# One token tile's up rows summed by TensorE, no fifth dense tile, and most expert activations made in the up stage

## The chip, the cores and the metric

The kernel runs on one core of one Trainium2 chip. The metric is the device time of one execution in microseconds; the number quoted for a kernel is the median over its timed runs. Beside these, one execution is recorded by the hardware profiler; its span runs from the first to the last instruction.

The core's engines work in parallel, each from its own in-order queue: TensorE (PE; its weight loads are PEld), VectorE (DVE), ScalarE (ACT), GpSimd (POOL) and SyncE (SP), which here only starts DMA transfers.

## The reference

One decoder layer for 1024 tokens of 1024 features, in fp32. A mixer (gated short convolution beside dilated attention, merged by gates) is followed by a retrieval layer over 16384 experts, and by a last normalisation:

```python
h = h + hybrid_mixer(rms_norm(h, norm_mix[layer]), ...)
h = h + peer_ffn(rms_norm(h, norm_ffn[layer]), w_query, sub_keys, expert_down, expert_up)
return rms_norm(h, final_norm)

# peer_ffn: each of 8 heads picks 16 experts for each token: 128 rows of each table
idx, gates = ...                     # (token, 128) expert numbers and their softmax weights
a = gelu(einsum('cd,ced->ce', xc, expert_down[ic]))    # 128 dot products per token
out = einsum('ce,ced->cd', gc * a, expert_up[ic])      # weighted sum of 128 up rows per token
```

The table `expert_down` (`down`) and the table `expert_up` (`up`) hold 16384 rows of 1024 numbers, 64 MiB each.

## The kernel before, in words

Tokens are handled in two halves of 512, and in tiles of 128 tokens (0 to 3 in the first half, 4 to 7 in the second). The whole program is written as Python generators that yield a cost; the instructions of two of them, a main line and a side line, are interleaved by these costs and the numbers `PACE_B`, `PACE_C`, `PACE_D`. A scheduler of the framework then fixes the order in each engine's queue, by its own estimate of when things are ready.

The main line: the mixer of the first half and its expert scores (**mixer 0**); the mixer of the second half and its scores (**mixer 1**); then `dense()`, which treats the experts of the second half without any gather. `dense()` has two stages:

- the **hidden stage**: `hidden(q)` multiplies the weights of 512 experts (`down_t`) with all 512 tokens and applies gelu; a group q takes 4 x 8 x 3 = 96 matmuls of 512 columns, because each fp32 product is made of three f32r products of a high and a low part (`mm3`, L176 to L178; `weights()` loads 512 KB into `raw`, ScalarE casts it to `hi`, VectorE subtracts to get `lo`, L163 to L167). There are 32 groups. The first `STORED` = 27 results are sent to DRAM (`a_d`), the next `HOLD` = 4 stay. Meanwhile `routes()` makes the gates: for each tile it chooses the experts on VectorE (`choose`), then `build` makes one-hot matrices of four tokens at a time (`oa`, `ob`), multiplies them on TensorE (`psg`), copies them on ScalarE (`stg`) and stores a full gate matrix in DRAM (`g_d`). `RATE_G` sets how fast the builder goes beside the hidden groups;
- the **up stage**: for each group q, `fetch(q)` reads the activations back, `weigh(q)` multiplies them with the gates `gg` read from `g_d` and splits them into `hh` and `hl`, and the rows of `up` are loaded (`rawu`), split (`uh`, `ul`) and multiplied, 24 matmuls for each tile. Six of the sums stay in PSUM for the whole stage (`held`), the others are added to SBUF by VectorE (`rest`, L1089).

The side line, `experts()`, treats the tiles of the first half by gathers: POOL fetches one of the 128 expert rows of each token (512 KB for a tile of 128 tokens) by an indirect DMA into one of `ROWS` = 4 buffers; VectorE makes the dot product (`row`, L875) or adds the scaled row to `acc` (`rowu`, L891). So a tile takes 128 gathers with dots and 128 with row sums. Tile 1 is an exception: its dots are made this way, but its up rows go through `dense()` as a fifth tile (`XT`, `given`), which takes its gates from the side line and needs `gx`, `xh`, `xl` in each up step.

POOL's queue holds all gathers and the small loads of the side line, SP's queue all other transfers.

Of the kernel before, what the change touches and what calls it, by code (L numbers as in the profile page):

```python
# [8 lines left out]
F32 = mybir.dt.float32  # L9
# [8 lines left out]
P = 128  # L18
# [15 lines left out]
PACE_B = 2.0  # L34
PACE_D = 2.0
PACE_C = 2.2
RATE_G = 0.8
STORED = 27
HOLD = 4
# [9 lines left out]
TILES = (4, 5, 6, 7, 1)  # L49
STB = 2  # L50
XT = (1,)
GXB = 2
XHB = 1
# [12 lines left out]
def hybrid_layer(ctx, tc, x, xT, pos, rotc, norm_mix, w_proj, w_v, conv_w, w_conv_out, w_attn_out,  # L66
                 gate_bias, w_out, norm_ffn, w_query, sub_keys, down, down_t, up, final_norm, out):
# [83 lines left out]
    s_d = dram.tile([3, P, 16, P], F32, name="s_d")  # L151
    a_d = dram.tile([STORED, P, NB, TH], F32, name="a_d")
    g_d = dram.tile([(TH + len(XT) * P) // TC, P, P, TC], F32, name="g_d")
# [540 lines left out]
    def tail(half, tiles, h1, sts, after):  # L694
# [32 lines left out]
        kept = tiles if half else [t for t in tiles if t == 0]  # L727
# [3 lines left out]
        for hc in range(16):  # L731
# [11 lines left out]
            if sent:  # L743
                others = w2k.tile([P, 3, P], F32, tag="t0", name="others")[:, 0:len(sent)]
                S.copy(others, pk[:, len(kept):nt])
                nc.sync.dma_start(s_d[sent[0] - 1:sent[-1], :, hc].rearrange("t p k -> p t k"), others)
# [86 lines left out]
    def stored(tt):  # L833
        part = {}

        def column(hc):
            if hc % 2 == 0:
                part[0] = ex.tile([P, 2, P], F32, tag="sv", bufs=2, name="sv")
                SIDE.dma_start(part[0], s_d[tt - 1, :, hc:hc + 2])
# [4 lines left out]
    later = [None] + [choose(stored(tt), False, picked) for tt in (1, 2, 3)]  # L844
# [14 lines left out]
    xready = {}  # L859

    def experts():
        for tt in ORDER:
            r = slice(tt * P, tt * P + P)
            if tt:
                for _ in later[tt]:
                    pass
            idx, gate = picked[tt]
            ut = ex.tile([P, D], F32, tag="ut", name="ut")
            SIDE.dma_start(ut, u2_d[r])
            a = ex.tile([P, P], F32, tag="a", name="a")  # L870
            for e in range(P):
                row = gt.tile([P, D], F32, tag="row", name="row")
                G.indirect_dma_start(out=row, out_offset=None, in_=down,  # L873
                                     in_offset=bass.IndirectOffsetOnAxis(ap=idx[:, e:e + 1], axis=0))
                V.tensor_tensor_reduce(out=row, in0=row, in1=ut, scale=1.0, scalar=0.0, op0=ALU.mult,  # L875
                                       op1=ALU.add, accum_out=a[:, e:e + 1])
                yield 1.0
            S.activation(a, a, AF.Gelu)
            if tt in XT:
                ax = ex.tile([P, P], F32, tag=f"ax{tt}", name="ax")  # L880
# [295 lines left out]
```

## Time and profile before

| | us |
|---|---|
| median of 3 timed runs (lowest, highest) | 3424.61 (3417.29, 3427.93) |
| the profiled execution, its own time | 3433.88 |
| its span, first to last instruction | 3432.1 |
| TensorE busy in it | 3274.4 |
| VectorE busy | 2760.1 |
| ScalarE busy | 1461.7 |
| POOL busy | 1190.2 |
| bytes moved by DMA | 948.08 MB |

Busy time is the time in which an engine executes at least one instruction. Matmuls follow each other in a pipeline, so what TensorE gets done is read from how many start in a stretch, not from its busy share alone. The granted TensorE clock has two levels, 1.2 and 2.4 GHz; its mean share over the span is 0.984.

### The profile page before, as it was taken

Reading aid. Unit: us, or ns where it says so; the run is one execution under the profiler, and the core shown is the slowest. Engines: PE = TensorE matmul, PEld = TensorE weight load, DVE = VectorE, ACT = ScalarE, POOL = GpSimd, SP = SyncE. Lnnn points to the kernel's source line nnn. Section 1 sums busy time; section 2 is a strip of 40 time slices with the busy share of each in tenths; the row PEclk is TensorE's granted clock in tenths of the full one; section 3 lists DMA queues with packets and bytes.
Section 4 is the critical chain, followed back from the end, with each engine's and each line's share of the span. In section 5 each row is a group of like instructions: output and inputs, shape, how many; then the busy total and the mean of one; then the engine's idle time right before and its main releaser. Section 6 shows DMA issues by size and latency. Waiting matters only on the chain.

```text
span 3432.1 us, 47074 instructions
## 1 busy us (share of the span) xinstructions
PE 3274.4 (95%) x15923; PEld 2685.0 (78%) x15923; DVE 2760.1 (80%) x5646; ACT 1461.7 (43%) x3271; POOL 1190.2 (35%) x944
## 2 busy tenths in 40 slices
PE   7999999999989999988999989999999999999998
PEld 6787888887767777767777878888877878787787
DVE  4333355689999889988999999998887878888887
ACT  3544444443334353333226777787632222222222
POOL 0000000014543345555434443464544334444342
PEclk9999999999989999989999999999999999999999
DMA  4233335668888678988889898999989989999895
GB/s 129 77 119 110 103 127 191 244 230 305 302 279 276 227 260 307 342 316 292 315 316 328 329 330 334 344 340 336 348 301 336 334 316 338 326 340 333 309 350 208
DMA packets 364307, 948.08 MB, mean 276 GB/s; under 512 B 33952, under 2 KB 127648, under 8 KB 356640
## 3 DMA queue, kind: packets, MB, share of 16 engines
q1 hardware_dynamic: 232016, 465.27, 38.9%
q0 software_dynamic: 132048, 479.78, 38.8%
q8 instruction: 126, 2.06, 0.2%
q14 instruction: 117, 0.96, 0.1%
HBM read 843.15 MB, written 95.49 MB: 273 GB/s over the span
## 4 chain that ended last, share of the span: by engine, by line
PE 32%; DVE 20%; DMA 14%; issue 11%; POOL 5%; ACT 1%; SPq 0%; DVEq 0%; POOLq 0%; ACTq 0%
DVE row L875 6%; PE ps L178 6%; PE ps L176 6%; PE ps L177 6%; DMA row<-in_down,idx 5%; DMA rowu<-in_up,idx 4%; DMA gg<-g_d 4%; DVE lo L167 3%; POOL row L873 3%; POOL rowu L889 2%; PE held L177 2%; PE held L178 2%; PE held L176 2%; DVE acc L891 1%; PE psg L975 1%
## 5 line engine op out<-in xcount | busy, mean ns | idle before, releaser
L873 POOL DMA_INDIRECT row<-in_down,idx x512 | 640.9, 1252 | 885.2 <-DVE a L875 465.6
L889 POOL DMA_INDIRECT rowu<-in_up,idx x384 | 525.8, 1369 | 621.1 <-DVE acc L891 499.0
L165 ACT CAST hi<-raw 128x1024 fp32r<-128x1024 f32 x368 | 387.6, 1053 | 746.0 <-PE ps L177 541.1
L875 DVE CUSTOM_DVE_ANT_0 row<-row,ut 128x1024 f32<-128x1024 f32 x512 | 618.8, 1215 | 79.2 <-DMA row<-in_down,idx 74.0
L167 DVE TENSOR_TENSOR lo<-raw,hi 128x1024 fp32r<-128x1024 f32 x368 | 448.1, 1218 | 247.9 <-ACT hi L165 238.6
L178 PE MATMUL ps<-vhi,lo 128*128 128x512 f32 (+1 forms) x1408 | 535.4, 382 | 33.5 <-DVE lo L167 33.4
L176 PE MATMUL ps<-vhi,hi 128*128 128x512 f32 (+1 forms) x1408 | 530.6, 377 | 10.8 <-ACT hi L165 6.7
L891 DVE SCALAR_TENSOR_TENSOR acc<-rowu,a,acc 128x1024 f32<-128x1024 f32 x384 | 491.2, 1279 | 59.7 <-DMA rowu<-in_up,idx 57.3
L177 PE MATMUL ps<-vlo,hi 128*128 128x512 f32 (+1 forms) x1408 | 528.9, 376 | 0.0
L178 PE MATMUL ps<-uhi,lo 128*128 128x512 f32 x1024 | 409.1, 400 | 4.2 <-DVE lo L167 4.2
L176 PE MATMUL ps<-uhi,hi 128*128 128x512 f32 x1024 | 407.6, 399 | 5.7 <-ACT uhi L181 3.1
L177 PE MATMUL ps<-ulo,hi 128*128 128x512 f32 x1024 | 409.1, 400 | 0.5 <-DVE ulo L182 0.5
L178 PEld LDWEIGHTS ps<-vhi,lo 128*128 128x128 f32 x1408 | 269.1, 191 | 87.4 <-DVE lo L167 44.4
L176 PEld LDWEIGHTS ps<-vhi,hi 128*128 128x128 f32 x1408 | 269.7, 192 | 58.9 <-ACT hi L165 10.9
L177 PEld LDWEIGHTS ps<-vlo,hi 128*128 128x128 f32 x1408 | 269.1, 191 | 45.1
L177 PE MATMUL held<-ul,hh 128*128 128x512 f32 x624 | 247.0, 396 | 11.1 <-DVE ul L182 10.9
L178 PE MATMUL held<-uh,hl 128*128 128x512 f32 x624 | 244.0, 392 | 2.5 <-DVE hl L182 2.5
L176 PEld LDWEIGHTS ps<-uhi,hi 128*128 128x128 f32 x1024 | 194.1, 190 | 52.1 <-ACT uhi L181 5.2
L176 PE MATMUL held<-uh,hh 128*128 128x512 f32 x624 | 233.3, 393 | 0.0
L178 PEld LDWEIGHTS ps<-uhi,lo 128*128 128x128 f32 x1024 | 194.3, 190 | 47.9 <-DVE lo L167 6.4
L177 PEld LDWEIGHTS ps<-ulo,hi 128*128 128x128 f32 x1024 | 194.1, 190 | 45.1 <-issue 3.0
L181 ACT CAST hh<-ga 128x512 fp32r<-128x512 f32 x128 | 71.4, 618 | 353.0 <-DVE ga L990 348.9
(347 smaller groups left out, 5947.8 us busy)
## 6 DMA issues: line engine op xcount, KB each, us to landing
raw<-in_w_proj SPq DMA_DIRECT2D x128, 512.0 KB
raw<-in_down_t SPq DMA_DIRECT2D x128, 512.0 KB
rawu<-in_up SPq DMA_DIRECT2D x128, 512.0 KB
g_d<-stg SPq DMA_DIRECT2D x80, 512.0 KB
gg<-g_d SPq DMA_DIRECT2D x32, 1024.0 KB
a_d<-ga SPq DMA_DIRECT2D x27, 1024.0 KB
ga<-a_d SPq DMA_DIRECT2D x27, 1024.0 KB
raw<-in_w_query SPq DMA_DIRECT2D x48, 512.0 KB
```

Of the source, the lines that this page charges most:

```text
L165: S.copy(hi, raw)
L167: V.tensor_tensor(lo, raw, hi.bitcast(F32), op=ALU.subtract)
L176: PE.matmul(ps, l[0], r[0], start=first, stop=False)
L177: PE.matmul(ps, l[0], r[1], start=False, stop=False)
L178: PE.matmul(ps, l[1], r[0], start=False, stop=last)
L181: S.copy(hi, src)
L873: G.indirect_dma_start(out=row, out_offset=None, in_=down, in_offset=bass.IndirectOffsetOnAxis(ap=idx[:, e:e + 1], axis=0))
L875: V.tensor_tensor_reduce(out=row, in0=row, in1=ut, scale=1.0, scalar=0.0, op0=ALU.mult, op1=ALU.add, accum_out=a[:, e:e + 1])
L889: G.indirect_dma_start(out=row, out_offset=None, in_=up, in_offset=bass.IndirectOffsetOnAxis(ap=idx[:, e:e + 1], axis=0))
L891: V.scalar_tensor_tensor(acc, row, a[:, e:e + 1], acc, op0=ALU.mult, op1=ALU.add)
L975: PE.matmul(ps[:, t], ob[:, t], oa[:, t], start=True, stop=True)
```

## The change

- The fifth dense tile is gone: `given`, `gx`, `xh`, `xl` are removed, `dense()` has four tiles. The side line takes tile 1's up rows by gathers and row sums like the others.
- Tile 0's up rows are gathered too, but by token instead of by rank: `turn_over` transposes its weights and expert numbers, so that one gather brings the 128 rows of one token, one per partition. `summed` lets TensorE add them: for four tokens at a time it multiplies the rows by a matrix `z` that is zero but for one column, into a strip of 32 output columns for each of the four, both halves of the features, 256 fp32 matmuls in all, over two PSUM tiles (`upacc`). Its rows use the four gather buffers and pairs of the large buffers (`rowb`) in turn. The up stage is not written before this sum is done (`while "done" not in place`).
- The side line's order is now given by `STEPS`: the dots of tiles 0, 1 and 2, then the sums of tiles 0 (TensorE), 1 and 2 (VectorE), then tile 3's dots and sums.
- `STORED` is 8 and `HOLD` is 2: 10 hidden groups are made in the hidden stage, 22 in the up stage, each one step before it is used.
- The gates `gg` have one buffer of their own, not one of the ten large ones; the scores of three tiles of the second half go through DRAM (`s_d`); `weigh` works on halves of 256 tokens; the rows of `up` are laid out on the host (`up_s`) so that a load is contiguous in each partition.
- The paces: the side line goes faster beside mixer 1, the builder faster beside the hidden groups.

```diff
-PACE_B = 2.0
-PACE_D = 2.0
-PACE_C = 2.2
-RATE_G = 0.8
-STORED = 27
-HOLD = 4
+PACE_B = 1.55
+PACE_D = 1.55
+PACE_C = 1.75
+RATE_G = 1.3
+STORED = 8
+HOLD = 2
...
-TILES = (4, 5, 6, 7, 1)
+STEPS = ((0, 0), (1, 0), (2, 0), (0, 1), (1, 1), (2, 1), (3, 0), (3, 1))
+TILES = (4, 5, 6, 7)
 STB = 2
-XT = (1,)
-GXB = 2
-XHB = 1
+SUMMED = 0
+ZK = 2
...
-            if tt in XT:
-                ax = ex.tile([P, P], F32, tag=f"ax{tt}", name="ax")
-                V.tensor_tensor(ax, a, gate, op=ALU.mult)
-                xready[tt] = (idx, ax)
...
+            if tt == SUMMED:
+                while not place:
+                    yield 1.0
+                acc = ex.tile([P, D], F32, tag="acc", name="acc")
+                yield from summed(*turned[tt], acc, r)
...
+        def add(s, rows):
+            z = zs[s // ZK % 2]
+            c0 = 31 + 32 * (s % ZK) - s
+            first = None
+            for n in range(2):
+                for j in (3, 0, 1, 2):
+                    with tc.issue_after(first.ins) if first else ExitStack():
+                        m = PE.matmul(part[n][32 * j:32 * j + 32], z[:, j, c0:c0 + 32], rows[j][:, n * TH:n * TH + TH],
+                                      start=s == 0, stop=s == 31)
+                    first = first or m
+
+        for s in range(32):
+            if s % ZK == 0:
+                S.copy(zs[s // ZK % 2][:, :, 31::32][:, :, 0:ZK], columns[:, :, s:s + ZK])
+            if s % 2:
+                pair = [m8.tile([P, 2, D], F32, tag="big", name="rowb") for _ in range(2)]
+                rows = [pair[j // 2][:, j % 2] for j in range(4)]
+            else:
+                rows = [gt.tile([P, D], F32, tag="row", name="rowu") for _ in range(4)]
+            for j in range(4):
+                t = 32 * j + s
+                G.indirect_dma_start(out=rows[j], out_offset=None, in_=up,
+                                     in_offset=bass.IndirectOffsetOnAxis(ap=iT[:, t:t + 1], axis=0))
+            if waiting:
+                add(*waiting.pop())
+            waiting.append((s, rows))
+            yield 4.0
...
-            gg = m8.tile([P, TH // TC, NB, TC], F32, tag="big", name="gg")
-            nc.sync.dma_start(gg, g_d[:TH // TC, :, NB * q:NB * q + NB].rearrange("c j i t -> j c i t"))
+            gg = up_p.tile([P, TH // TC, NB, TC], F32, tag="gg", bufs=1, name="gg")
+            nc.sync.dma_start(gg, g_d[:, :, NB * q:NB * q + NB].rearrange("c j i t -> j c i t"))
...
         for _ in builder:
             yield 0.0
+        while "done" not in place:
+            next(side)
...
-                    r0 = (NB * q + ii) * P
-                    nc.sync.dma_start(raw, up[r0:r0 + 2 * P, n * TH:n * TH + TH].rearrange("(a p) d -> p a d", a=2))
+                    nc.sync.dma_start(raw, up_s[(NB * q + ii) // 2, n])
```

Two places show where the instructions stand now. The first is TensorE's queue at the end of the hidden stage of the kernel before: `ps` are hidden matmuls (the last of L176 to L178), `psg` the gate builds, and the numbers tell buffers apart.

```order
L178 MATMUL ps<-vhi_12767,lo 128x512
L975 MATMUL psg<-oa,ob 128x128 x4
L176 MATMUL ps<-vhi_12767,hi 128x512
L177 MATMUL ps<-vlo_12769,hi 128x512
L178 MATMUL ps<-vhi_12767,lo 128x512
L176 MATMUL ps<-vhi_12766,hi 128x512
L177 MATMUL ps<-vlo_12768,hi 128x512
```

In the changed kernel the same stage ends with these rows; `upacc` are the sums over strips (8 matmuls for four tokens), `rowu` and `rowb` their gathered rows, `ps_t` the transposes with which the last tile's gates begin, `held` the first matmuls of the up stage.

```order
L178 MATMUL ps<-vhi_13012,lo 128x512
L1038 MATMUL psg<-oa,ob 128x128 x8
L944 MATMUL upacc<-rowu,z_13826 32x512 x8
L944 MATMUL upacc<-rowb,z_13826 32x512 x8
L1038 MATMUL psg<-oa,ob 128x128 x24
L944 MATMUL upacc<-rowu,z_13827 32x512 x8
L944 MATMUL upacc<-rowb,z_13827 32x512 x8
L1038 MATMUL psg<-oa,ob 128x128 x32
L1015 MATMUL ps_t<-ident,e_17743 128x128 x2
L1015 MATMUL ps_t<-ident,ge 128x128
L1038 MATMUL psg<-oa,ob 128x128 x128
L176 MATMUL held_18912<-uh,hh 128x512
```

Before, the last builds stood between hidden matmuls, and more hidden ones followed them; now the `upacc` sums stand in the queue in sixteens, and the last 184 builds have no hidden matmul beside or behind them.

The other place is VectorE's queue in one step of the up stage, from the product with the gates (`ga<-ga,gg`) on; `row,a` is a dot of a gathered row, `a` its second half. Before:

```order
L990 TENSOR_TENSOR ga_26741<-ga_26741,gg_26743 128x512 x4
L182 TENSOR_TENSOR ul_26326<-rawu_26323,uh_26325 128x1024
L1089 TENSOR_TENSOR rest_22594<-rest_22594,psu_26289 128x512
L182 TENSOR_TENSOR ul_26416<-rawu_26413,uh_26415 128x1024
L1089 TENSOR_TENSOR rest_22594<-rest_22594,psu_26290 128x512
L875 ISA row_23887,a_21908<-row_23887,ut_21906 128x1024
L875 ISA a_21908 128x1
L875 ISA row_23896,a_21908<-row_23896,ut_21906 128x1024
```

In the changed kernel, with the last `lo` split of a hidden group ahead of the product:

```order
L167 TENSOR_TENSOR lo_24374<-raw_24370,hi_24372 128x1024
L1056 TENSOR_TENSOR ga_23981<-ga_23981,gg_24152 128x4x256 x2
L887 ISA row_22674,a_22287<-row_22674,ut_22285 128x1024
L887 ISA a_22287 128x1
L887 ISA row_22683,a_22287<-row_22683,ut_22285 128x1024
L887 ISA a_22287 128x1
L182 TENSOR_TENSOR hl_24155<-ga_23981,hh_24154 128x4x256 x2
L887 ISA row_22706,a_22287<-row_22706,ut_22285 128x1024
L887 ISA a_22287 128x1
L182 TENSOR_TENSOR ul_24256<-rawu_24253,uh_24255 128x1024
L1146 TENSOR_TENSOR rest_18914<-rest_18914,psu_24174 128x512
```

The `lo` splits of the hidden groups have moved into the up stage, between the dots, and each dot waits in this queue for its gathered row.

## Rows read from the trace of the kernel before

**Rows 1.** The page: busy time by engine; the chain that ended last.
```profile
PE 3274.4 (95%) x15923; PEld 2685.0 (78%) x15923; DVE 2760.1 (80%) x5646; ACT 1461.7 (43%) x3271; POOL 1190.2 (35%) x944
PE 32%; DVE 20%; DMA 14%; issue 11%; POOL 5%; ACT 1%; SPq 0%; DVEq 0%; POOLq 0%; ACTq 0%
```

**Rows 2.** Busy time by stretch: four stages, three of 100 us.
```profile
core 0: us, PE busy (x) PEld busy (x) DVE busy (x) ACT busy (x) POOL busy (x), PEclk, DMA share, GB/s
0.00:750.00 750.00, 720.71 (x3650) 589.20 (x3651) 382.44 (x910) 338.77 (x659) 5.30 (x17) 0.99 0.43 142
750.00:1580.00 830.00, 772.15 (x3921) 625.60 (x3920) 750.81 (x1822) 318.42 (x608) 385.27 (x325) 0.96 0.85 292
1580.00:2480.00 900.00, 860.80 (x4381) 723.79 (x4380) 844.66 (x1876) 563.42 (x1666) 415.31 (x305) 0.99 0.90 329
2480.00:3432.00 952.00, 920.71 (x3976) 746.39 (x3974) 782.24 (x1040) 241.10 (x339) 384.36 (x299) 0.99 0.88 318
1700.00:1800.00 100.00, 92.16 (x397) 73.67 (x397) 93.09 (x287) 28.36 (x36) 39.99 (x35) 1.00 0.89 314
2700.00:2800.00 100.00, 100.00 (x438) 82.02 (x437) 83.01 (x125) 25.56 (x34) 36.44 (x30) 1.00 0.91 329
3000.00:3100.00 100.00, 99.89 (x435) 81.05 (x434) 83.81 (x104) 20.94 (x29) 43.68 (x35) 1.00 0.95 345
```

**Rows 3.** Groups by line: busy us, mean ns of one, idle before, releasers.
```profile
L873 POOL DMA_INDIRECT row<-in_down,idx x512 | 640.9, 1252 | 885.2 <-DVE a L875 465.6 <-DVE tv L762 115.6 <-issue 35.6
L875 DVE CUSTOM_DVE_ANT_0 row<-row,ut 128x1024 f32<-128x1024 f32 x512 | 618.8, 1215 | 79.2 <-DMA row<-in_down,idx 74.0 <-issue 4.0 <-DMA ut<-u_d 0.9
L167 DVE TENSOR_TENSOR lo<-raw,hi 128x1024 fp32r<-128x1024 f32 x368 | 448.1, 1218 | 247.9 <-ACT hi L165 238.6 <-DMA raw<-in_w_proj 4.2 <-PE pst L548 2.1
L891 DVE SCALAR_TENSOR_TENSOR acc<-rowu,a,acc 128x1024 f32<-128x1024 f32 x384 | 491.2, 1279 | 59.7 <-DMA rowu<-in_up,idx 57.3
L975 PE MATMUL psg<-oa,ob 128*128 128x128 f32 x1280 | 162.0, 279 | 8.5 <-ACT stg L977 5.9 <-DVE ob L968 1.9 <-ACT ob L973 0.7
L977 ACT COPY stg<-psg 128x128 f32<-128x128 f32 x640 | 126.0, 286 | 61.8 <-PE psg L975 29.9 <-DMA g_d<-stg 22.9 <-issue 7.8
L966 ACT ACTIVATE ob<-iota,sT 128x128 f32<-128x128 f32 x320 | 103.9, 416 | 0.2
L967 ACT ACTIVATE ob<-ob,ones 128x512 f32<-128x512 f32 x80 | 60.7, 764 | 0.1
L1089 DVE TENSOR_TENSOR rest<-rest,psu 128x512 f32<-128x512 f32 x120 | 80.4, 679 | 2.0 <-PE psu L178 2.0
```

**Rows 4.** TensorE in time: start us, us, line, out<-in, count.
```profile
166.46 1.09 PE L504 MATMUL pv<-pts,v_t 128*64 128x128 f32 x16
...
508.71 1.02 PE L244 MATMUL prs<-diag,ones 128*128 128x512 f32 x2
509.81 0.39 PE L178 MATMUL ps<-uhi,lo 128*128 128x512 f32 x1
```

**Rows 5.** POOL's gathers by stage: of `in_down` (L873), then of `in_up` (L889).
```profile
1580.00:2480.00 900.00, 267.47 (x213) 0.99 0.90 329
2480.00:3432.00 952.00, 165.14 (x128) 0.99 0.88 318
...
1580.00:2480.00 900.00, 147.27 (x91) 0.99 0.90 329
2480.00:3432.00 952.00, 215.81 (x165) 0.99 0.88 318
```

**Rows 6.** Who waited for whom in the up stage: us, times, longest.
```profile
DVE ga L990 <- DMA gg<-g_d: 73.3, 26, 8.4
```

**Rows 7.** All engines in order of time around 1749 us.
```profile
1748.07 1.22 DVE L875 CUSTOM_DVE_ANT_0 row<-row,ut 128x1024 f32<-128x1024 f32 x1 [2.50 <-DMA row<-in_down,idx]
1749.22 1.22 DVE L167 TENSOR_TENSOR lo<-raw,hi 128x1024 fp32r<-128x1024 f32 x1
1750.49 0.50 PE L178 MATMUL ps<-vhi,lo 128*128 128x512 f32 x1 [2.68 <-DVE lo L167]
```

More of the change, by code (lines that the diff above doesn't have):

```diff
@@ L724, in tail @@
             result["next"] = mixer(1)
-        kept = tiles if half else [t for t in tiles if t == 0]
+        kept = [t for t in tiles if t == 0]
         sent = [t for t in tiles if t not in kept]
@@ L856, in finish, with new_row @@
             queue.dma_start(out[r, c], acc[:, c])
[L859 removed]
+    place = {}
+    spare = []
+    count = [0]
+    def new_row(name):
+        pools = [gt] * ROWS + spare
+        pool = pools[count[0] % len(pools)]
+        count[0] += 1
+        return pool.tile([P, D], F32, tag="row", name=name)
     def experts():
[L862 removed]
+        values, turned = {}, {}
+        for tt, side_up in STEPS:
             r = slice(tt * P, tt * P + P)
[L864 to L894 removed]
@@ new lines, in experts @@
+            if not side_up:
+                for _ in later[tt] or ():
+                    pass
+                idx, gate = picked[tt]
+                ut = ex.tile([P, D], F32, tag="ut", name="ut")
+                SIDE.dma_start(ut, u2_d[r])
+                a = ex.tile([P, P], F32, tag="a", bufs=3, name="a")
+                for e in range(P):
+                    row = new_row("row")
+                    G.indirect_dma_start(out=row, out_offset=None, in_=down,
+                                         in_offset=bass.IndirectOffsetOnAxis(ap=idx[:, e:e + 1], axis=0))
+                    V.tensor_tensor_reduce(out=row, in0=row, in1=ut, scale=1.0, scalar=0.0, op0=ALU.mult,
+                                           op1=ALU.add, accum_out=a[:, e:e + 1])
+                    yield 1.0
+                S.activation(a, a, AF.Gelu)
+                V.tensor_tensor(a, a, gate, op=ALU.mult)
+                values[tt] = (idx, a)
+                if SUMMED in values and SUMMED != tt and SUMMED not in turned:
+                    turned[SUMMED] = turn_over(*values[SUMMED])
+                continue
@@ new lines, in experts @@
+            idx, a = values[tt]
+            st = ex.tile([P, 3], F32, tag="st", name="st")
+            if tt == SUMMED:
+                while not place:
+                    yield 1.0
+                acc = ex.tile([P, D], F32, tag="acc", name="acc")
+                yield from summed(*turned[tt], acc, r)
+            else:
+                acc = ex.tile([P, D], F32, tag="acc", name="acc")
+                SIDE.dma_start(acc, h1_d[r])
+                for e in range(P):
+                    row = new_row("rowu")
+                    G.indirect_dma_start(out=row, out_offset=None, in_=up,
+                                         in_offset=bass.IndirectOffsetOnAxis(ap=idx[:, e:e + 1], axis=0))
+                    V.scalar_tensor_tensor(acc, row, a[:, e:e + 1], acc, op0=ALU.mult, op1=ALU.add)
+                    yield 1.0
@@ L902, in dense @@
         mix.close()
+        side_p = ctx.enter_context(tc.tile_pool(name="side", bufs=1))
+        zs = [side_p.tile([P, 4, 32 * ZK + 31], F32, name=f"z{k}") for k in range(2)]
+        for z in zs:
+            G.memset(z, 0.0)
+        place["zs"] = zs
         bld = ExitStack()
@@ L1104, in hybrid_layer @@
         pass
[L1105 removed]
+    side = experts()
     due = 0.0
```

90 lines of the change are left out of this document (43 added, 47 removed).

## The prediction

> **What bounds it now.** I read the busy shares and the chain of waits first. TensorE is busy 95% of the span, VectorE 80%, and the chain that ended last is shared by TensorE (32%), VectorE (20%) and DMA (14%) [rows 1]: no engine holds the whole run, so I went by stage. Mixer 0 (0 to 750 us) has no expert rows yet. In mixer 1 (B, 830 us), the hidden stage (C, 900 us) and the up stage (D, 952 us) three resources are near full at once: VectorE is busy 0.90, 0.94 and 0.82 of the three, the DMA engines 0.85, 0.90 and 0.88, TensorE 0.93 to 0.97 [rows 2]. What TensorE can do at most is seen in a hundred us of D in which it never waits: 438 matmuls, 0.228 us each. A stretch of the hidden stage without builds gets only 397 [rows 2].
>
> The sum is made against the profiled execution: span 3432.1, its own time 3433.9 us. The median of the timed runs is 3424.6, 9.3 below; the last step takes that off.
>
> **The change, stage by stage.** Counts of instructions are from code and order, durations from rows. A hidden group is 96 matmuls of 512 columns, a dense tile 24 per up step. A gather brings 0.524 MB.
>
> *Mixer 0*: nothing but order inside the query: 750.
>
> *Mixer 1*: TensorE's work is the same. With the new paces VectorE's order has 345 gathered rows here, where it had 309: 36 dots of 1.215 + 0.08 us [rows 3], 47 us. VectorE idles 79 of 830 us [rows 2], scattered between waits. Lower bound 0 (all of it falls into that idle time), upper 47 (none does, and each delays a `lo` split for which TensorE waits). I take about half: 852. The DMA engines get 22 MB on top of 242, 310 GB/s, no more than elsewhere.
>
> *Hidden stage*, by difference from C's 900 us, each engine alone:
> - TensorE: 10 hidden groups, not 31: 960 x 0.228 = 219 us. Builds: 162 us for five tiles [rows 3], so 130. The 256 new sums over strips of 32 columns, in fp32, are in no trace. A full-width fp32 matmul of 512 columns is two passes; from its start to the start of the second f32r matmul behind it are 1.10 us, less one f32r 0.87 [rows 4]: 256 x 0.87 = 223 us if the four strips run in turn, 56 if all four run at once. The nearest row is the attention's value product, which writes two 64-column strips alternately: 16 passes in 1.09 us, where 16 passes of that length at full width cost 16 x 0.127 = 2.0 [rows 3, 4]. So two strips do run together; I take that half, 111. Sum 460, bounds 405 and 572.
> - VectorE: 845 busy before; less 84 `lo` splits (102), 164 dots (212), 50 row sums (64) and 64 build operations at the 0.68 of a 128x512 operation (44) [rows 3]: 423. At C's 0.94 that is 450 us.
> - DMA: 329 x 900 = 296 MB [rows 2]; less 84 weight loads of 0.524 MB (44), 19 activations not written (20), 16 gate pieces (8) and 86 gathers (45; 304 before [rows 5]), plus 3 for scores read back: 182 MB. At 345 GB/s, the best hundred us of D, 527 us; at C's own 329, 553 [rows 2].
> - The end: 184 of the 512 build matmuls (46 steps of four tokens) stand in TensorE's order behind nearly the last hidden one. ScalarE paces such a step: by busy time over count 4 copies of 0.197 and either 4 activations of 0.325 with one of 0.76, or 4 scalings that I price like the activations [rows 3], on average 2.5 us, so 114 us in which TensorE has little. It is no extra as long as gathers fill it: VectorE's order has 41 row sums of the next tile there, 21 MB, beside 12 MB of gates. It lies inside the 527.
>
> The DMA engines' 527 is the largest and stands. Under it, up to 527 x 0.956 (C's TensorE share) - 349 = 155 us of strip matmuls hide; run in turn they would add 70 us. The Trainium skill (TensorE: Matmul & The Clock Gate, Part 3) measures 2.38x for three column strips at once; by it the 223 us would be some 94, an estimate, and the sum the same. No row here has more than two strips.
>
> *Up stage*, by difference from D's 952 us:
> - TensorE: before, 32 x 120 + 96 = 3936 matmuls x 0.228 = 897, so 55 us of start, end and gaps. After, 32 x 96 + 22 x 96 = 5184: 1182, and with the same 55: **1237**. This term decides.
> - VectorE: 782 [rows 2]; less 60 adds to `rest` (41) and 32 `xl` at the same price (22); plus 84 `lo` (102) and 178 more row sums (228) [rows 3]: 1049 of 1237, 0.85, where it had 0.82. Covered, with less to spare.
> - DMA: 318 x 952 = 303 MB; plus 84 weight loads (44) and 178 gathers (93; 293 before [rows 5]), less 19 activations read (20) and `gx` (8): 412 MB, in 1237 us 333 GB/s, between D's mean of 318 and its best hundred of 345 [rows 2]. Rows of `up` now come in pieces of 4 KB, not 2; I count nothing for it.
> - `gg` has one buffer of its own: its load, and SP's queue behind it (weight loads among them), waits until the product of the step before has read it. Today VectorE waits 73.3 us for `gg` in 26 places [rows 6]. The load may now come a step early, or hold SP up; between a gain of 73 and a like loss I take 0.
> - POOL issues 128 gathers more, at 1.25 to 1.31 us [rows 3, 5]: 165 us on 1190 in a span of 3400. It stays under half busy.
>
> Sum: 750 + 852 + 527 + 1237 = 3366 of span, 3368 with what lies around it, less 9: **about 3360 us**, 1.9% faster. TensorE loses 768 matmuls of 512 columns (175 us); more than half of it is not gained, because they go where VectorE and the DMA engines are as full as TensorE.
>
> **Rivals.**
> 1. *The rows come no faster than today.* After mixer 0 the DMA engines carry 22 - 114 + 109 = 17 MB more than before. If C stays at 329 and D at 318 GB/s: 750 + 852 + 553 + 1295 = 3450 of span, **3443**, slower. For it: they are busy 0.88 to 0.90, and no stage was faster on average. Against it: 345 over a hundred us, and POOL's idle time before a gather is mostly VectorE's doing [rows 3], not DMA's. The point is 325 GB/s in the up stage: 412 / 0.325 = 1268 leaves a gain, 412 / 0.318 none. The Trainium skill (DMA: Bandwidth & Descriptors, Issuing engines are not separate DMA queues) has transfers of all queues share the same 16 engines; by that rule POOL's gathers and SP's loads add up as I add them, and the stages of before, at 292 to 329 GB/s with unlike mixes of the two, agree.
> 2. *Hidden matmuls starve in the up stage.* Two weight buffers of 24 matmuls stand between TensorE and VectorE's queue, which now holds some 16 dots or row sums per step. One late row shows what follows: the dot at 1748.07 waited 2.50 us for its gather, the `lo` behind it was late, and TensorE stood 2.68 us [rows 7]. At the hidden stage's 397 per hundred us [rows 2]: 5184 / 3.97 = 1306, with 35 for start and end 1341; 3470 of span, **3463**, slower. Against it: that stretch also held choosing, with VectorE 0.93 busy; here it is 0.85. The point is 410 matmuls per hundred us; below it nothing is gained.
> 3. *The DMA engines do more than they ever had to, and the `gg` wait goes.* Up stage 1182 + 20, hidden stage 505 (360 GB/s), mixer 1 845: 3302 of span, **3295**. For it: VectorE, not DMA, is what POOL waits for today. Against it: no hundred us above carries 360.
>
> **Numbers.** Forecast 0.55, its own range 3315 to 3420; rival 3 0.15; rival 1 0.16; rival 2 0.14. A measurement here tells 0.3% (10 us) from no change: under 3414 is faster, over 3435 slower. Of the forecast 0.04 lies within that, and of rival 1, which has values between the forecast and its 3443, 0.06. Faster 0.51 + 0.15 = 0.66; same 0.10; slower 0.10 + 0.14 = 0.24. The range takes in rival 1, most of rival 3 and the ends of the terms (mixer 1 +25, strip matmuls in turn +70, `gg` 73 either way, not all at once): 3280 to 3445. What is left out is most of rival 2 and the far side of rival 3.
>
> **What would show it.** Right: an up stage near 1237 us with 420 or more matmuls per hundred us at some 330 GB/s; a hidden stage near 527 us at 340 GB/s or more; strip matmuls starting in groups, not 0.43 us apart; mixer 1 at 850. Rival 2: under 410 matmuls, with TensorE's longest waits on `lo`. Rival 1: DMA engines full and VectorE waiting for `row` and `rowu`. Wrong altogether: a hidden stage above 600 us or a mixer 1 above 880, since there I have taken VectorE and the DMA engines to have room.

## The result, and the profile after

The changed kernel takes 3443.65 us (median of 6 runs, 3438.23 to 3452.64), the kernel before 3426.27 beside it: ratio 1.0057, interval 1.0031 to 1.0083. It is 0.6% slower. The profiled execution took 3448.45 us, its span is 3446.7.

The page of the changed kernel, busy time by engine and the chain that ended last (before: [rows 1]):

```profile
PE 3165.5 (92%) x15410; PEld 2559.9 (74%) x15410; DVE 2669.4 (77%) x5357; ACT 1398.0 (41%) x2898; POOL 1422.7 (41%) x1101
PE 29%; DMA 16%; issue 14%; DVE 12%; POOL 9%; ACT 2%; SPq 1%; POOLq 0%; DVEq 0%; ACTq 0%
```

TensorE is busy 109 us less than before, in a longer span; DMA's share of the last chain is up from 14 to 16%, POOL's from 5 to 9%. Busy time by stretch (before: [rows 2]): four stages, then the hidden stage in four parts, then two stretches of the up stage.

```profile
core 0: us, PE busy (x) PEld busy (x) DVE busy (x) ACT busy (x) POOL busy (x), PEclk, DMA share, GB/s
0.00:750.00 750.00, 723.03 (x3685) 591.92 (x3686) 385.65 (x925) 340.53 (x662) 8.90 (x19) 0.99 0.45 143
750.00:1594.00 844.00, 775.84 (x3889) 624.90 (x3888) 784.65 (x2009) 332.75 (x596) 436.32 (x361) 0.95 0.89 311
1594.00:2188.00 594.00, 468.13 (x2656) 364.87 (x2654) 467.03 (x1350) 370.59 (x1234) 283.49 (x243) 0.90 0.85 309
2188.00:3446.00 1258.00, 1198.52 (x5184) 978.15 (x5184) 1032.03 (x1075) 354.17 (x406) 693.98 (x481) 0.98 0.92 327
1594.00:1757.00 163.00, 117.26 (x559) 98.39 (x557) 154.97 (x477) 77.29 (x220) 81.00 (x73) 0.88 0.88 309
1757.00:2070.00 313.00, 293.69 (x1774) 213.50 (x1774) 219.39 (x757) 207.04 (x683) 142.87 (x128) 0.97 0.85 315
2070.00:2175.00 105.00, 57.00 (x327) 52.98 (x323) 87.09 (x115) 85.38 (x329) 53.22 (x38) 0.77 0.81 286
2175.00:2200.00 25.00, 0.19 (x2) 0.00 (x0) 16.20 (x14) 5.76 (x10) 12.46 (x10) 0.56 0.99 359
2300.00:2400.00 100.00, 100.00 (x439) 82.24 (x439) 82.15 (x71) 26.68 (x29) 55.71 (x39) 1.00 0.93 341
3000.00:3100.00 100.00, 94.04 (x401) 75.85 (x400) 78.79 (x111) 25.81 (x30) 58.58 (x41) 0.98 0.92 324
```

Predicted were 750, 852, 527 and 1237 us; measured are 750, 844, 594 and 1259 (the hidden stage is counted to 2188, where the first `gg` is loaded; the first up matmul comes at 2200). The hidden stage misses by 67, the up stage by 22. The four parts show why no average over the hidden stage tells its length. Up to 1757 the experts are chosen: VectorE is busy 155 of 163 us. Up to 2070 tile 0's rows are summed over strips, TensorE 0.94 busy. From then on only the last gates are left: TensorE has 57 us of work in 105, its granted clock is down to 0.77 (a mean of its two levels), and for the last 25 us it has none. Each resource is full somewhere and idle elsewhere.

Who waited for whom, first in the hidden stage (1594 to 2200), then in the up stage (from 2188): us in all, times, longest. [Rows 6] have the wait for `gg` before.

```profile
POOL rowu L958 <- PE upacc L944: 118.1, 15, 13.5
...
PEld psg L1038 <- ACT stg L1040: 48.4, 23, 6.9
...
PE psg L1038 <- DVE ob L1031: 29.5, 10, 6.1
...
DVE acc L910 <- DMA rowu<-in_up,idx: 121.7, 91, 5.5
...
DVE row L887 <- DMA row<-in_down,idx: 53.1, 40, 3.7
...
PE held L176 <- ACT hh L181: 24.9, 1, 24.9
...
PE ps L178 <- DVE lo L167: 12.0, 9, 3.6
...
DVE ga L1056 <- DMA gg<-g_d: 1.8, 1, 1.8
```

The wait for `gg` is gone, 73.3 to 1.8 us, but VectorE now stands 175 us at its queue's head for gathered rows. With 1032 us of work that makes 1207 of the stage's 1258: VectorE is the second full engine there. In the hidden stage POOL stands 118 us for strips before it can gather again. The groups that answer to [rows 3], line by line:

```profile
L887 DVE CUSTOM_DVE_ANT_0 row<-row,ut 128x1024 f32<-128x1024 f32 x512 | 618.1, 1216 | 94.9 <-DMA row<-in_down,idx 89.3 <-issue 3.4 <-DMA ut<-u_d 1.3
...
L910 DVE SCALAR_TENSOR_TENSOR acc<-rowu,a,acc 128x1024 f32<-128x1024 f32 x384 | 492.4, 1282 | 141.6 <-DMA rowu<-in_up,idx 132.1 <-DMA acc<-h_d 5.7
...
L1038 PE MATMUL psg<-oa,ob 128*128 128x128 f32 x1024 | 157.9, 316 | 80.0 <-ACT stg L1040 42.7 <-DVE ob L1031 29.5 <-ACT ob L1036 5.7
```

The wait for up rows is 132 us, where it was 57. Last, two groups of strip matmuls in time, with the first and last start:

```profile
L944 PE MATMUL upacc<-rowu,z x16: 592/592/617, 1817.0 to 1818.4; 128*32 128x512 f32 x16
L944 PE MATMUL upacc<-rowb,z x16: 592/592/592, 1818.8 to 1820.1; 128*32 128x512 f32 x16
```

16 passes are 8 matmuls (two passes each in fp32). The second group starts 1.8 us after the first: 0.23 us a matmul, where one alone was priced at 0.87. All 256 keep TensorE busy for 62 us.

### The profile page after: what moved, and what is told of

The parts are those of the page before. It is cut to its first block, busy times and chain, and to the rows that moved or that the text cites. A ratio compares the mean times of both kernels' runs of the same rounds, so it can differ in the third digit from the quotient of the medians.

```text
span 3446.7 us, 45451 instructions
## 1 busy us (share of the span) xinstructions
PE 3165.5 (92%) x15410; PEld 2559.9 (74%) x15410; DVE 2669.4 (77%) x5357; ACT 1398.0 (41%) x2898; POOL 1422.7 (41%) x1101
## 4 chain that ended last, share of the span: by engine, by line
PE 29%; DMA 16%; issue 14%; DVE 12%; POOL 9%; ACT 2%; SPq 1%; POOLq 0%; DVEq 0%; ACTq 0%
DMA rowu<-in_up,idx 7%; POOL row L885 6%; PE ps L178 5%; PE ps L176 5%; PE ps L177 5%; DMA row<-in_down,idx 4%; DVE row L887 4%; POOL rowu L908 3%; PE held L176 2%; PE held L177 2%; PE held L178 2%; PE psg L1038 2%; DVE lo L167 1%; PE upacc L944 1%; DVE acc L910 1%
## 5 line engine op out<-in xcount | busy, mean ns | idle before, releaser
L885 POOL DMA_INDIRECT row<-in_down,idx x512 | 668.9, 1306 | 670.9 <-DVE a L887 331.2
L908 POOL DMA_INDIRECT rowu<-in_up,idx x384 | 559.1, 1456 | 456.9 <-DVE acc L910 392.8
L178 PE MATMUL ps<-vhi,lo 128*128 128x512 f32 (+1 forms) x1408 | 531.4, 377 | 29.1 <-DVE lo L167 27.4
L176 PE MATMUL ps<-vhi,hi 128*128 128x512 f32 (+1 forms) x1408 | 527.3, 375 | 5.8 <-ACT ga L989 3.6
L176 PE MATMUL ps<-uhi,hi 128*128 128x512 f32 x1024 | 407.0, 399 | 7.8 <-ACT hi L165 5.3
L178 PE MATMUL ps<-uhi,lo 128*128 128x512 f32 x1024 | 407.7, 399 | 2.0 <-DVE lo L167 1.9
L178 PEld LDWEIGHTS ps<-vhi,lo 128*128 128x128 f32 x1408 | 267.9, 190 | 84.5 <-DVE lo L167 34.7
L176 PE MATMUL held<-uh,hh 128*128 128x512 f32 x752 | 290.2, 395 | 24.9 <-ACT hh L181 24.9
L176 PEld LDWEIGHTS ps<-vhi,hi 128*128 128x128 f32 x1408 | 268.0, 190 | 54.8 <-ACT ga L989 5.3
L177 PE MATMUL held<-ul,hh 128*128 128x512 f32 x752 | 297.1, 395 | 5.3 <-DVE ul L182 5.3
L178 PE MATMUL held<-uh,hl 128*128 128x512 f32 x752 | 294.9, 393 | 0.0
L181 ACT CAST uh<-rawu 128x1024 fp32r<-128x1024 f32 x126 | 131.6, 1049 | 380.6 <-DMA rawu<-in_up_s 310.8
L176 PEld LDWEIGHTS ps<-uhi,hi 128*128 128x128 f32 x1024 | 193.3, 189 | 54.5 <-ACT hi L165 7.8
L1038 PE MATMUL psg<-oa,ob 128*128 128x128 f32 x1024 | 157.9, 316 | 80.0 <-ACT stg L1040 42.7
```

The costliest lines, as they stand in the source:

```text
L176: PE.matmul(ps, l[0], r[0], start=first, stop=False)
L177: PE.matmul(ps, l[0], r[1], start=False, stop=False)
L178: PE.matmul(ps, l[1], r[0], start=False, stop=last)
L181: S.copy(hi, src)
L885: G.indirect_dma_start(out=row, out_offset=None, in_=down, in_offset=bass.IndirectOffsetOnAxis(ap=idx[:, e:e + 1], axis=0))
L908: G.indirect_dma_start(out=row, out_offset=None, in_=up, in_offset=bass.IndirectOffsetOnAxis(ap=idx[:, e:e + 1], axis=0))
```

## The experiments

18 kernels ran. Two theories stood first: **1**, each part of the hidden stage has its own full engine, and TensorE bounds the up stage; **2**, the bytes bound both. Others came as these failed: **3**, both limits stand close together; **4**, the four row buffers set the pace of the gathers; for the strip sum **5**, a loop through TensorE's queue, or **6**, the gathers' own rate. "Main line" and "side line" are those of the kernel's description. The table has for each kernel the ratio to the kernel before with its interval, and from the trace the hidden stage (first `down_t` load to first up matmul), the start of the last up matmul and that of VectorE's last row sum, in us.

| kernel | ratio | hidden | last matmul | last row sum |
|---|---|---|---|---|
| changed kernel | 1.0057 (1.0031, 1.0083) | 606 | 3419 | 3434 |
| stored14 | 1.0153 (1.0125, 1.0180) | 675 | 3352 | 3474 |
| stored20 | 1.0257 (1.0229, 1.0285) | 752 | 3284 | 3501 |
| bal14 | 1.0194 (1.0171, 1.0217) | 693 | 3368 | 3487 |
| nosum | 1.0335 (1.0309, 1.0361) | 626 | 3449 | 3525 |
| noload | 1.0227 (1.0210, 1.0245) | 614 | 3498 | 3383 |
| quarter | 1.0252 (1.0232, 1.0271) | 590 | 3505 | 3403 |
| skip | 1.0077 (1.0054, 1.0100) | 603 | 3241 | 3450 |
| skipq | 1.0036 (1.0019, 1.0053) | 599 | 3309 | 3424 |
| r5 | 1.0076 (1.0050, 1.0101) | 585 | 3372 | 3438 |
| r6 | 1.0038 (1.0022, 1.0055) | 586 | 3367 | 3424 |
| b14r6 | 1.0097 (1.0070, 1.0124) | 697 | 3352 | 3444 |
| s14r6 | 1.0011 (0.9997, 1.0026) | 674 | 3327 | 3413 |
| s11r6 | 1.0050 (1.0031, 1.0069) | 634 | 3349 | 3421 |
| hquarter | 1.0096 (1.0071, 1.0122) | 622 | 3450 | 3435 |
| hskip | 1.0096 (1.0063, 1.0130) | 600 | 3426 | 3458 |
| d3 | 1.0077 (1.0054, 1.0101) | 624 | 3444 | 3433 |
| hskip3 | 1.0043 (1.0025, 1.0061) | 603 | 3421 | 3426 |
| d3s14r6 | 1.0009 (0.9998, 1.0020) | 694 | 3345 | 3420 |

### More hidden groups in the hidden stage: stored14, stored20, bal14

```diff
-RATE_G = 1.3
-STORED = 8
+RATE_G = 0.85    # stored20: 0.65
+STORED = 14      # stored20: 20
```

bal14 is stored14 with `PACE_C` 1.6 and `PACE_D` 1.45.

> Theory 1 (phases): the hidden stage of the changed kernel (594 us) is a row of phases with a bound each, choosing on VectorE (163 us, TensorE busy 117), strips on TensorE (313 us), the last tile's route weights on ScalarE and VectorE (118 us, TensorE busy 57), so some 126 us of TensorE lie idle in it. Six groups more done there (14 in place of 8 stored, 576 hidden matmuls, 131 us by 0.228) take some of that idle time: hidden stage 640 to 670, up stage down from 1259 to about 1120, whole run 3370 to 3400. Theory 2 (the run goes by the bytes that DMA moves): the six groups add 12 MB of writing and reading of stored activations to 965 MB, so the run gets longer, 3455 to 3490.

> Twelve groups more stored than in the changed kernel (1152 hidden matmuls, 263 us by 0.228). Theory 1 (phases): more than the idle 126 us of TensorE, so the second half fills nothing: hidden stage 740 to 780, up stage about 980, whole run 3350 to 3400, no better than with 14 by more than 15 us. Theory 2 (bytes): 25 MB more, 3475 to 3530.

> 14 groups stored, as in the run where the main line ended 108 us before the expert rows, with the rows called 7 to 9% oftener (paces 1.6 and 1.45 in place of 1.75 and 1.55), so that both end together. Theory 1 (the rows were only called too late; DMA has room): main line still ends near 3380, rows too, whole run 3385 to 3410, under both kernels. Theory 2 (the rows come no faster, since DMA is full): 609 MB from 1603 us on at 330 GB/s are 1845 us, whole run 3440 to 3470, with the main line held back by rows that come late.

Stored14 in stretches: hidden stage, its last part, up stage, and the end:

```profile
1604.00:2279.00 675.00, 584.09 (x3233) 456.33 (x3231) 530.49 (x1403) 413.44 (x1288) 321.37 (x267) 0.93 0.88 323
2092.00:2254.00 162.00, 153.56 (x852) 133.34 (x852) 141.04 (x164) 127.08 (x416) 73.30 (x58) 0.98 0.92 338
2279.00:3352.00 1073.00, 1059.78 (x4606) 865.87 (x4607) 876.74 (x916) 305.15 (x338) 598.43 (x395) 1.00 0.93 331
3375.00:3470.00 95.00, 0.00 (x0) 0.00 (x0) 64.73 (x53) 0.00 (x0) 55.30 (x50) 0.50 0.84 285
```

Inside the main line theory 1 holds: 576 more matmuls (131 us) lengthen the hidden stage by 69, because the last gates now have matmuls beside them (TensorE busy 154 of 162 us), at 338 GB/s. The last matmul comes 67 us earlier. In stored20 the hidden stage is 752 us, as it said, and the last matmul 135 us earlier. The runs are slower all the same, 3482 and 3514 us, inside theory 2's ranges; but the place is not where bytes would put it: for 95 us at the end of stored14 only rows are gathered and added, at 285 GB/s. bal14 was to call them oftener; its 3495 us lie above both ranges. Counted in VectorE's queue, 312 of the 384 row sums stand ahead of the main line's last split of `up` rows in stored14 and 313 in bal14 (367 in the changed kernel). So the pace of the calls did not move them; that the scheduler's own estimate puts them there is an inference, and bal14 does not tell what rows placed earlier would do.

### The strip sum taken back: nosum

```diff
-SUMMED = 0
+SUMMED = -1
...
-        while "done" not in place:
+        while SUMMED >= 0 and "done" not in place:
```

> One part undone: tile 0's up rows are summed by VectorE as those of tiles 1 to 3 (128 accumulations of 1.28 us, 164 us, more for VectorE; 256 strip matmuls, 64 us, fewer for TensorE; the same bytes). Theory 1 (phases): the stretch from the end of choosing to the end of the route weights loses the 64 us of TensorE, but VectorE, 467 us busy in the hidden stage, gets up to 164 more there, so hidden stage 600 to 650 and whole run 3450 to 3500. Theory 2 (bytes): the same bytes, whole run within 10 us of 3444.

Hidden stage 626, run 3539: slower than theory 1 said, and theory 2 is out. The strip sum is a part of the change that pays: without it, the run loses 2.8% more. No other part of the change was undone by itself.

### Bytes and matmuls out of the up stage: noload, quarter, skip, skipq

In quarter a load fills a quarter of its buffer, which is read four times; noload reads one fixed piece; skip drops one pass; skipq is quarter and skip.

```diff
-                ps = project(weights(down_t[NB * q + ii]), U2)
+                ps = project(weights(down_t[NB * q + ii], 8, q >= STORED + HOLD), U2)      # quarter
+                ps = project(weights(down_t[NB * q + ii]), U2, skip=q >= STORED + HOLD)    # skip
...
+        if quarter:
+            nc.sync.dma_start(raw[:, 0:2], src[:, 0:2])
+            raw = raw[:, 0:2][:, None].to_broadcast([P, 4, 2, P])
...
-        PE.matmul(ps, l[0], r[1], start=False, stop=False)
+        if not skip:
+            PE.matmul(ps, l[0], r[1], start=False, stop=False)
```

> The 22 groups whose hidden matmuls run in the up stage use one fixed piece of weights in place of loading their blocks of down_t (46 MB of the stage's 412 MB are left out; their split into two parts stays, and the output differs). Theory 1 (TensorE bounds the up stage: 1198 busy of 1259 us): up stage 1225 to 1250, whole run 3415 to 3440. Theory 2 (bytes bound it): 46 MB at the 330 GB/s of the stage are 139 us, up stage 1120 to 1140, whole run 3305 to 3330.

> In the up stage the 88 loads of down_t bring a quarter of their bytes (34.6 MB of the stage's 411 MB are left out; the quarter is used four times, so the output differs; every wait, buffer and engine operation stays). Theory 1 (TensorE bounds the up stage: 1198 busy of 1259 us): its last matmul stays within 15 us of 3419, and only the rows' waits fall; whole run 3425 to 3445. Theory 2 (bytes bound it): 34.6 MB at 327 GB/s are 106 us, whole run 3335 to 3360.

> The hidden groups of the up stage leave out one of their three matmul passes, weight part hi with activation part lo (22 x 32 = 704 matmuls of 0.235 us, 165 us of TensorE; the output differs; all loads, splits and rows stay). Theory 1 (TensorE bounds the up stage): its last matmul 130 to 165 us earlier; the whole run can't gain all of it, since the rows then end last as with 14 stored groups, 3340 to 3400. Theory 2 (bytes bound it): 411 MB at no more than 340 GB/s are 1208 us, so whole run 3395 to 3445.

> Both together: 704 matmuls and 34.6 MB fewer in the up stage. Theory 1 (TensorE alone bounds it): as with the 704 matmuls alone, within 15 us. Theory 2 (bytes alone bound it): as with the 34.6 MB alone, within 15 us. Theory 3 (both are at their limit, so that either alone gives little): well below both, 3270 to 3310.

Fewer bytes make it slower, outside the ranges of both theories. Waits in quarter's up stage:

```profile
DVE acc L915 <- DMA rowu<-in_up,idx: 126.5, 97, 5.2
...
PE ps L183 <- DVE lo L172: 63.9, 20, 6.4
DVE row L892 <- DMA row<-in_down,idx: 50.1, 47, 2.9
```

With 371 MB to move in place of 411, VectorE waits 177 us for rows, as in the changed kernel (175): a lighter load on the DMA engines does not bring them sooner. What changed is VectorE's queue: all 384 row sums now stand ahead of its last split, not 367, the `lo` splits come later, and TensorE waits 64 us for them (12 in the changed kernel). noload shows the same (last matmul 3498), and once its rows are done TensorE runs 431 matmuls in 100 us with 69 GB/s moving. So theory 2 gets no support here, but these two kernels are no clean subtraction: the scheduler laid their queues out anew. What speaks against it more plainly is r6, below, which moves 341 GB/s in the same stage.

Skip does what theory 1 says of TensorE and nothing for the run. Its up stage, and 180 us after it:

```profile
2205.00:3241.00 1036.00, 1030.40 (x4479) 843.28 (x4480) 872.74 (x917) 344.35 (x393) 553.63 (x369) 1.00 0.95 335
3260.00:3440.00 180.00, 0.00 (x0) 0.00 (x0) 121.26 (x96) 0.00 (x0) 109.17 (x94) 0.50 0.83 280
```

The last matmul comes 178 us earlier (130 to 165 expected), at 335 GB/s, and the run ends no sooner than the changed kernel's. At the end 94 gathers take 180 us, 1.91 each, with VectorE (121 us) and POOL (109) both idle in between and hardly anything else on the DMA engines. Of skipq, theory 3 expected far less than either alone; it is 0.4% above the kernel before, in none of the three ranges.

### More row buffers in the up stage: r5, r6, b14r6, s14r6, s11r6

The strip operands' space is freed before the up stage and goes to one more row buffer (r5), or two with one buffer for split `up` rows fewer (r6). b14r6, s14r6 and s11r6 are r6 with bal14, with stored14, and with `STORED` 11 (`RATE_G` 1.0).

```diff
-UPS = 7
+UPS = 6
...
         bld.close()
+        strips.close()
+        spare.extend([ctx.enter_context(tc.tile_pool(name="more", bufs=2))] * 2)
```

> The changed kernel with a fifth row buffer in the up stage (in the place of the strip matmuls' operands, which are no longer needed there), nothing else. Theory 4 (the rows go round four buffers: issue 1.4 us, landing 7.0, row sum 1.28, so a row every 2.4 us at best, and VectorE stands 169 us of the up stage at its queue's head for late rows): five buffers allow one per 1.9, VectorE's waits for rows fall below 85 us, whole run 3395 to 3430. Theory 2 (the DMA engines, busy 0.92, carry no more): the landing grows with the rows in flight, from 7.0 to about 9 us, VectorE's waits stay within 30 us of 169, whole run 3434 to 3454.

> As with five row buffers, but six in the up stage, and one buffer fewer (six for seven) for the split rows of up. Theory 4: waits for rows below 50 us, whole run 3385 to 3425, unless the buffer taken from the splits costs some of it. Theory 2: landing about 10 us, waits as before, whole run 3434 to 3460.

> 14 groups stored with the denser row calls (3495 us with four row buffers, where the main line ended 94 us before the rows) and six row buffers in the up stage. Theory 4: rows and main line end within 30 us of each other, whole run 3380 to 3420, which would beat both kernels. Theory 2: 609 MB after 1603 us at 330 GB/s, 3440 to 3490.

> 14 groups stored at the changed kernel's own paces (3482 us with four row buffers; main line done at 3375) and six row buffers in the up stage. Theory 4: main line done by 3365, the rows' tail after it, 51 rows of 1.9 us, shrinks to 1.4 us a row or some 70 us, whole run 3420 to 3450. Theory 2: within 15 us of 3482.

> 11 groups stored and six row buffers in the up stage, between two runs that stand: 8 and six (3435 us, main line's last matmul at 3367) and 14 and six (3428, 3327). If the rows' line alone sets the end by now, the last matmul comes at 3340 to 3355 and the whole run still takes 3420 to 3440, no better than the kernel before by more than 5 us. If main line and rows still trade, 3400 to 3420.

r6: the up stage to its last matmul, and the rows' end after it, then waits in the whole stage, VectorE's for up rows last:

```profile
2180.00:3367.00 1187.00, 1186.73 (x5183) 975.01 (x5184) 1012.31 (x1029) 346.92 (x396) 668.81 (x478) 1.00 0.95 341
...
3380.00:3425.00 45.00, 0.00 (x0) 0.00 (x0) 40.93 (x36) 0.00 (x0) 30.44 (x27) 0.50 0.98 377
```

```profile
POOL rowu L908 <- DVE acc L910: 330.8, 187, 13.9
...
DVE lo L167 <- ACT hi L165: 114.1, 56, 6.0
...
DVE acc L910 <- DMA rowu<-in_up,idx: 10.2, 11, 2.3
```

The mechanism of theory 4 is right: VectorE's waits for rows fall from 175 to 77 us with five buffers and to 11 with six, TensorE is busy 1186.7 of 1187 us, and its 5184 matmuls take 1187 us, not 1219, while the DMA engines move 341 GB/s, and 377 when only rows are left. The size is wrong: r5 gains nothing in the run and r6 0.2%, with intervals that overlap the changed kernel's, because the side line now ends 57 us behind the last matmul in r6. Both times lie in theory 2's ranges, but the waits that it said would stay are gone. Of the 384 row sums, 338 stand ahead of r6's last split. VectorE's longest wait is now 114 us at `lo` for ScalarE's `hi`, which itself waits for matmuls (276 us), and the row sums behind `lo` in VectorE's queue wait with it; POOL stands 331 us for row sums. With 14 groups stored the same two buffers give 1.4% (stored14 1.0153, s14r6 1.0011, in theory 4's range) and make up what the change lost, no more. b14r6, 3460 us, lies in theory 2's range, with its hidden stage 23 us longer than s14r6's; why the denser calls cost that was not followed up. In s11r6 the side line alone sets the end, as the first reading said; why s14r6, with a longer hidden stage, still ends 10 us sooner (3428 against 3438) it does not explain.

### What holds the hidden stage: hquarter, hskip, d3, hskip3, d3s14r6

hquarter and hskip are quarter and skip with `q < STORED + HOLD` as condition. d3 gives the strip sum twelve row buffers; hskip3 adds it to hskip, d3s14r6 to s14r6.

```diff
-            if s % 2:
+            if s % 3:
...
-            if waiting:
-                add(*waiting.pop())
+            if len(waiting) == 2:
+                add(*waiting.pop(0))
```

> In the hidden stage (not in the up stage) the 40 loads of down_t bring a quarter of their bytes (15.7 of the stage's 183.5 MB are left out; the output differs). Theory 1 (phases: choosing on VectorE, strips on TensorE, the last route weights on ScalarE and VectorE): hidden stage 580 to 605 us, as it was (594), at a lower DMA rate of some 285 GB/s. Theory 2 (bytes bound the hidden stage at 309 GB/s): 51 us less, 535 to 550. The up stage does the same work in both.

> The ten hidden groups of the hidden stage leave out one of their three matmul passes (320 of 960 matmuls, 80 us of TensorE by 0.25; the output differs; all loads and splits stay). Theory 1 (phases): only the strip phase is TensorE's, with 598 of the 960 matmuls, so 199 fewer there, 50 us; choosing and the end stay: hidden stage 535 to 560. Theory 2 (bytes): 183.5 MB as before, hidden stage 585 to 600.

> The changed kernel with twelve row buffers for the strip sum in place of eight: three steps of four rows in flight, and the strip matmuls of a step called two steps behind its gathers. In all runs so far that sum takes 306 to 324 us for its 128 rows, even with 320 fewer hidden matmuls. Theory 5 (a loop: a row buffer comes free only when TensorE, in its queue, has done the step's strips, and POOL waits some 118 us for that before it issues the next gathers): POOL's wait falls below 60 us, the strip phase (313 us) to 285 to 300, no lower, since TensorE is 294 busy in it; whole run 3420 to 3440. Theory 6 (the gathers themselves come no faster than one in 2.45 us): phase 306 to 324, whole run as the changed kernel.

> The same twelve row buffers together with the 320 matmuls fewer in the hidden stage (one of three passes of its ten groups left out, the output differs). Alone the fewer matmuls left the strip phase at 316 us with TensorE 261 busy in it. Theory 5 (loop): both limits are relaxed, phase 250 to 285. Theory 6 (gather rate): 306 to 324 again.

> 14 groups stored, six row buffers in the up stage (3428 us without the next edit) and the twelve row buffers for the strip sum. Theory 5: the rows' line, which ends last, starts its next rows 15 to 30 us earlier, whole run 3395 to 3415, faster than the kernel before. Theory 6: within 8 us of 3428.

The strip sum in hskip:

```profile
1768.00:2084.00 316.00, 261.19 (x1567) 180.34 (x1566) 223.82 (x769) 214.84 (x710) 133.39 (x128) 0.91 0.84 317
```

With 15.7 MB fewer hquarter's stage takes 622 us at 288 GB/s, longer and not shorter: bytes alone don't bound it. Its queues came out anew too (choosing ends after 134 us, not 163), so it is no clean subtraction. And 320 matmuls fewer bring only 6 us, where theory 1 said some 50 (theory 2's range for this run holds): the strip sum takes 316 us with TensorE 261 busy. Part of theory 1 falls with it: TensorE is nearly full in that part, but relieving it does not shorten it. Both taken out together were not tried here. Twelve buffers, d3: its strip sum, the middle of it, and the last of its gates:

```profile
1754.00:2053.00 299.00, 290.17 (x1706) 201.58 (x1708) 207.02 (x699) 191.50 (x614) 139.62 (x129) 0.99 0.87 322
...
1800.00:2035.00 235.00, 235.00 (x1346) 168.47 (x1345) 162.47 (x547) 152.90 (x482) 101.51 (x96) 1.00 0.88 326
...
2053.00:2216.00 163.00, 69.13 (x383) 63.09 (x375) 124.83 (x152) 106.77 (x401) 71.88 (x56) 0.71 0.81 283
```

The sum is 13 us shorter, POOL's wait for strips is still 120 us (78.4 and 41.6), and 56 passes of gate builds that stood in the sum now come after it: the stage is 18 us longer. With TensorE relieved as well, hskip3 takes 291 us for the sum, 25 fewer than hskip, between the ranges of both theories; d3s14r6 is level with s14r6, as theory 6 has it, with a hidden stage 20 us longer. So the loop of theory 5 costs 13 to 25 us. That the gathers themselves can come no faster, as theory 6 says, does not fit the trace of the changed kernel. TensorE's wait for rows in the whole strip sum, then the first and the last of eight gathers, and the next one:

```profile
PE upacc L944 <- DMA rowu<-in_up,iT: 9.3, 2, 6.6
...
1848.34 0.96 POOL L958 DMA_INDIRECT rowu<-in_up,iT  x1 [11.08 <-PE upacc L944]
...
1857.68 1.36 POOL L958 DMA_INDIRECT rowb<-in_up,iT  x1 [0.31 <-issue]
1867.68 1.93 POOL L958 DMA_INDIRECT rowu<-in_up,iT  x1 [8.64 <-PE upacc L944]
```

The eight are issued 1.3 us apart, then POOL stands 8.64 us until strips have freed buffers, while strips wait for rows only 9.3 us in all. In d3 TensorE has no gap from 1800 to 2035: with twelve buffers its queue is full there. So in these two kernels the rows wait for TensorE's queue, and hardly TensorE for rows. What holds the sum in hskip and hskip3, where TensorE has gaps (30 and 19 us of them for rows), is not settled.

## Why the prediction was wrong

**The step that failed** is in the hidden stage: "each engine alone", "the DMA engines' 527 is the largest and stands", and of the last builds, "it lies inside the 527". The bytes were right (183.5 MB, 182 predicted), and so was the price of a step of builds at the end (2.5 us predicted; 327 passes, some 40 steps of eight, in 105 us). TensorE's total was right by luck (468 us busy, 460): builds took 158 us where 130 were predicted, strips 62 where 111 were. But these totals don't lie under one another. The stage is a row in time: choosing 163 us, the sum of tile 0's 128 rows 313, the last gates 105, the first product with the gates 25, together 606 to the first up matmul. The largest total of an engine is only a lower bound, and nothing filled the gaps: in the last part the gathers that were to do so left the DMA engines at 286 GB/s, and in TensorE's queue all ten hidden groups stand ahead of the last 192 builds. At the prediction's 345 GB/s the bytes of the first three parts would have taken 146, 286 and 87 us, so that 17, 27 and 18 of the 67 us were lost in them (the rest goes with 1.5 MB more than predicted): the most in the strip sum, whose cause is in part open (above). stored14 shows that the gaps were real: 131 us of TensorE work cost 69. The change took the hidden groups out of the end of the stage, where before they had been the filling.

The 67 us are most of the 80 by which the sum of the stages missed (3366 predicted, 3446 measured). That a shorter hidden stage alone would have brought them is not shown: r5 has it 21 us shorter and ends no sooner, by what no case had (below). The time, 3443.65 us, lies at the very end of the widest range, 3280 to 3445, which took in rival 1; the forecast's own range ended at 3420.

**The up stage** was sized nearly right, 1237 for 1259. The term 5184 x 0.228 = 1182 is what r6 takes (1187); with four row buffers it is 1219, since VectorE stands 175 us for rows and its splits wait behind them; that start and end took 39 us and not 55 hides nearly half of it. The prediction had VectorE's work right (1049, measured 1032) and called it "covered, with less to spare"; it did not count an in-order queue's waits as load. The bytes were right (412 predicted, 411 moved).

**Rival 1** has the time (3443) by luck: it put the hidden stage at 553 and the up stage at 1295 us, which took 594 and 1259, two errors that cancel. It has not the mechanism either. VectorE does wait for `row` and `rowu`, as it said, and the hidden stage got 309 GB/s. But the DMA engines were not at their end in the up stage: two buffers bring 341. **Rival 2** did not come: the stage runs 5184 matmuls in 1219 us, 425 per hundred, not 397. Of **rival 3** only the `gg` part and mixer 1 (845, measured 844) came.

**What no case had**, the second step that failed: the sum follows the main line alone ("This term decides"), but the side line is an end of its own. The up stage holds 472 gathers, against 293 before [rows 5]; they take 2.7 us each (1258 / 472). The two lines end 15 us apart in the changed kernel, so a shorter main line brings nothing: 67 us less in stored14, 178 in skip, 92 in s14r6, and no run faster than the kernel before. Right were mixer 1 (844, predicted 852) and the strips in groups; and of what the text named as "wrong altogether", a hidden stage above 600 us, it is 594 by the prediction's boundary and 606 to the first up matmul.

**Open** is whether row sums placed earlier in VectorE's queue would let both lines end sooner: the pace did not move them, and no other order was tried. Open, too, is what the parts of the change other than the strip sum are worth one by one.

## What to carry to other kernels

Add up a stage as a sequence in time, with the engine that is full in each part; the largest total of an engine over the stage is a lower bound, and work moved out of it may have been the filling of its gaps. With two lines of work that share in-order queues, ask which ends last after the change, and count what a queue's head waits for as load. A buffer more in a ring of slow transfers is cheap to try before bandwidth is blamed. And work or bytes taken out of a kernel can change the order of its queues as well: quarter, with 35 MB less to load, is 2% slower than the changed kernel, with all its row sums ahead of the last split. Count the order before the times are compared.

## What the runs showed of the hardware

- Four 32-column fp32 strips run at once nearly in full: the strip matmuls of a group start 0.23 us apart, and all 256 keep TensorE busy for 62 us, against 0.87 us worked out for one at full width [rows 4]; 111 us were predicted. The Trainium skill (TensorE: Matmul & The Clock Gate, Part 3) has 2.38 times for three; no run here has three, and four give 3.8 by these two numbers.
- Gathers of 0.524 MB with hardly anything else on the DMA engines: four buffers give one in 1.91 us (280 GB/s, skip), with POOL waiting 53.5 of 180 us for row sums; six give one in 1.45 (38 in 55 us, 360 GB/s, s14r6). The next lines are POOL's in these two stretches:

```profile
L909 POOL DMA_INDIRECT rowu<-in_up,idx x94 | 109.7, 1167 | 72.2 <-DVE acc L911 53.5 <-issue 11.0 <-DMA rowu<-in_up,idx 6.3
...
L908 POOL DMA_INDIRECT rowu<-in_up,idx x38 | 42.5, 1118 | 12.5 <-issue 11.3 <-DVE acc L910 1.2
```

With six, POOL waits 1.2 us for buffers and issues nearly all of the time (42.5 us busy and 11.3 of issue in 55); with VectorE at 49 us of work in 55, it is no longer the buffers that set the rate.
